# Turning the first up block of each MLP by transposing transfers that start from SBUF

## The chip, the cores and the metric

The program runs on one NeuronCore of a Trainium2 chip. The metric is device time in microseconds from the start to the end of one execution, taken as the median over runs; lower is better. Five engines work side by side, each through its own list of instructions in order: PE (TensorE, matrix products), ACT (ScalarE), DVE (VectorE), POOL (GpSimd) and SP (SyncE, which here only issues transfers). Transfers are also issued by POOL. They are carried out by 16 DMA engines.

## The reference, cut to what matters

The reference is a two-layer decoder trunk on 256 rows (tokens) of 2048 values: attention, cross attention into 256 memory rows, and an MLP per layer, each on a normalised input and added to a residual stream. The change touches the MLP alone:

```python
D_MODEL, SEQ, DEPTH, D_FF = 2048, 256, 2, 4 * 2048

def sq_relu_mlp(h, wup, wdown):
    return jnp.square(jax.nn.relu(h @ wup)) @ wdown

x = x + sq_relu_mlp(rms_norm(x, mlp_norm[i]), mlp_wup[i], mlp_wdown[i])
```

All values are 32-bit floats.

## The kernel before, in words

**Products.** Every matrix product is made of three reduced-precision products: a 32-bit operand is split into a high half (a cast, on ACT) and a low half (operand minus high half, on DVE), and PE adds high·high, high·low and low·high into PSUM. So every weight tile of 128 x 2048 words that lands in a buffer called `raw` passes through ACT (`whi`, L221) and DVE (`wlo`, L222), in two pieces of 1024, before PE can use it. There are seven raw buffers, and four buffers each for the high and the low pieces, so ACT and DVE can be at most four pieces ahead of PE.

**Weight transfers.** The raw tiles are loaded on SP's queue in program order (`load`, L189). Some tiles get a second tile added by an accumulating transfer on POOL's queue (L879). A helper, `tc.keep_in_program_order`, ties an instruction to its place in its own queue.

**The MLP.** The 8192 hidden columns are cut into eight blocks of 1024, each of two halves of 512. Of block 0 both halves are made by plain products: an "up" chunk has four items (four raw tiles, 24 matmuls of 128x512 each) and its result stands in two PSUM banks called `mm`, one per row tile t of 128 rows. Blocks 1 to 7 are made with Strassen's scheme, seven products instead of eight (`Seven`; PSUM banks called `pr`; each product p1 to p7 has two items x0 and x1 of 12 matmuls). A "down" item multiplies a finished hidden half by one raw tile of the second weight (24 matmuls).

**The order on PE.** PE's list is written out by hand and kept as it is. `mlp_line` (from L1131) makes it: items of `Seven` in a fixed order, and between them, at the places that `SPREAD` names, items of block 0's second half and down items of finished blocks. A down item may be placed only when the hidden half that it reads counts as usable. Around block 1 the list reads: p1x0, p1x1, up item 0 (second half of block 0), p5x0, p5x1, up 1, p6x0, up 2, p3x0, p6x1, up 3, p3x1, then the first down item, which reads the first half of block 0, then p2x0, and the second down item, which reads the second half. The second half counts as usable 6 places after its last up item.

**The order on the other engines.** ACT, DVE, POOL and SP get their order from a scheduler that plays the program forward with its own estimates; the program gives it tasks that say, by a number after `yield`, how long to wait before the next step is put into the program.

**From an up chunk to a down item.** The hidden values leave PSUM with rows on the partitions and must be turned so that hidden columns are on the partitions. `out` (L1450) does it for one row tile and half: Relu with the row's scale, a square (L1457, L1458, both ACT), then one of two ways. One goes through memory: ACT copies the 512 words into two planes of 16-bit halves (`half_words`, L377), POOL stores the planes to HBM (L379), SP issues a transposing transfer back into SBUF (`turned_by_dma`, L384), which puts the two 16-bit halves of a word side by side again, and ACT and DVE split the landed words into high and low halves (`split_landed`, L390, L391). The other goes through PE: four 128x128 transposes into a PSUM bank (`transpose4`, which calls `flip`, L174), then `split` (L366, L367). Before the change the first half of block 0 takes the way through memory, and the second half takes the way through PE. Each half has two row tiles, and there are two layers, so each way is used four times.

Of the kernel before, what the change touches and what calls it, by code (L numbers as in the profile page):

```python
# [10 lines left out]
F32 = mybir.dt.float32  # L11
F32R = mybir.dt.float32r
I32 = mybir.dt.int32
U16 = mybir.dt.uint16
# [4 lines left out]
P = 128  # L19
# [3 lines left out]
CH = 512  # L23
# [4 lines left out]
LAST = MLP_BLOCKS - 1  # L28
SEVEN = (1, 2, 3, 4, 5, 6, 7)
SPREAD = {("p1", 1), ("p5", 1), ("p6", 0), ("p6", 1), ("p2", 0), ("p2", 1), ("p7", 1)}  # L30
EVS = 7
# [3 lines left out]
T_EV, T_TURN, T_ROT, T_SM, T_SQ, T_ADD, T_NORM, T_SUM, T_BATCH, T_STORE, T_LAND, T_DMA, T_SHORT = 2.6, 2.6, 12.0, 6.5, 4.4, 2.2, 7.2, 3.0, 17.0, 22.0, 7.0, 8.0, 11.0  # L35

URGENT = 250
NEG = -1.0e30
LAMBDA_INIT = 0.8 - 0.6 * math.exp(-0.3 * 0)
SC_DA = 1.0 / math.sqrt(128)  # L40
# [12 lines left out]
def trunk(ctx, tc, x, xT, xT0, mem, memT, positions, gcols, gfinal, lam_vecs, consts, W, out):  # L53
    nc = tc.nc

    def pool(name, bufs, space=None):
        kw = {"space": space} if space else {}
        return ctx.enter_context(tc.tile_pool(name=name, bufs=bufs, **kw))
# [5 lines left out]
    work = pool("work", 2)  # L64
# [6 lines left out]
    def nm(s):  # L71
        serial[0] += 1
        return f"{s}_{serial[0]}"

    def unit():
        return units.tile([P, 2, 4, S], F32R, tag="unit", name=nm("unit"))
# [79 lines left out]
    def side_bank():  # L156
        while not free_banks[0]:
            yield 0.5
        free_banks[0] -= 1
        return bank()  # L160

    def give_back():
        free_banks[0] += 1
# [12 lines left out]
    def f32(ap):  # L176
        return ap.bitcast(F32)
# [6 lines left out]
    def urgent():  # L184

        return tc.high_priority(offset=URGENT)

# [174 lines left out]
    def split(dst, t, src):  # L362

        n = src.shape[1]
        hi = dst[:, 0, :n, t * P : (t + 1) * P]
        nc.scalar.copy(hi, src)  # L366
        nc.vector.tensor_tensor(dst[:, 1, :n, t * P : (t + 1) * P], src, f32(hi), ALU.subtract)  # L367
# [7 lines left out]
    def half_words(src):  # L375
        planes = work.tile([P, 2, CH], U16, tag="ev", name=nm("planes"), padded_shape=[P, 2, CH], bufs=EVS)
        nc.scalar.copy(planes, src.bitcast(U16).rearrange("p (w s) -> p s w", s=2))  # L377
        there = turned.tile([2 * P, CH], U16, tag="turned", name=nm("turned"))
        nc.gpsimd.dma_start(there.rearrange("(q s) w -> q s w", s=2), planes)  # L379
        return there  # L380

    def turned_by_dma(there):
        landed = work.tile([P, 4, 2 * P], U16, tag="ev", name=nm("landed"), bufs=EVS)
        tc.keep_in_program_order(nc.sync.dma_start_transpose(landed, there))  # L384
        return landed.bitcast(F32).rearrange("p k t -> p k t")

    def split_landed(dst, t, src):
        at = slice(t * P, (t + 1) * P)
        hi = dst[:, 0, :, at]
        tc.keep_in_program_order(nc.scalar.copy(hi, src))  # L390
        nc.vector.tensor_tensor(dst[:, 1, :, at], src, f32(hi), ALU.subtract)  # L391

    def transpose4(src, pt):

        for k in range(4):
            flip(pt[:, k * P : (k + 1) * P], src[:, k * P : (k + 1) * P])
        return pt.rearrange("p (k t) -> p k t", k=4)
# [711 lines left out]
    def mlp_line(l):  # L1109

        def up(b, h):
            return Chunk(l, "up", [(b, h)]).items()

        def both(b, *more):
            return [(b, 0), (b, 1), *more]

        groups = [both(b) for b in range(MLP_BLOCKS)]

        def down(i):
            pairs = ((0, 1), (2, 3)) if (LAST - i) % 2 == 0 else ((2, 3), (0, 1))
            chunks = [Chunk(l, "down", groups[i], c, open=i == 0) for c in pairs[0]]
            chunks += [Chunk(l, "down", groups[i], c, close=False) for c in pairs[1] if i < LAST - 2 or c == 3]
            return [i for c in chunks for i in c.items()]

        line = up(0, 0)
        rest = up(0, 1) + [i for b in range(LAST - 1) for i in down(b)]
        seven = [i for b in SEVEN for i in Seven(l, b).items()]

        usable = {(0, 0): 0}  # L1131
        now, owed = 0, 0
        for item in seven:
            line.append(item)
            now += 1
            b = item.of.b
            if item.u == ("p4", 1):
                usable.update({(b, h): now + 6 for h in range(2)})
            owed += item.u in SPREAD or (b, item.u) == (1, ("p3", 1))
            while owed and rest:  # L1140
                of, u = rest[0].of, rest[0].u
                if of.kind == "down" and usable.get(of.halves[u], math.inf) > now:
                    break
                if of.kind == "up" and u == 3:
                    usable[of.halves[0]] = now + 6
                line.append(rest.pop(0))
                now += 2
                owed -= 1
        assert not rest
        plain = [  # L1150
            i
            for c in (3, 0, 1, 2)
            for i in Chunk(l, "down", both(LAST - 2, *both(LAST - 1)) if c == 2 else both(LAST - 1), c, open=c != 3).items()
        ]
        forms = {}
        pairs = {k: Pair(f"mlp_wdown{l}", 8 * LAST, 2, c, forms) for k, c in (("A", (0, 1)), ("B", (2, 3)))}
        end = []
        at = {}
        for word in CLOSING.split():
            at[word] = len(end)  # L1160
            if word == "u":
                end.append(plain.pop(0))
            else:
                of, p = pairs[word[0]], "p" + word[1]
                end.append(Item(of, p, [of.job(p)]))
        assert not plain
        steps = {}

        def put(i, do):
            steps.setdefault(i, []).append(do)  # L1170

        pairs["B"].by_sides = l == 1
        put(0, lambda hid: pairs["A"].sums([k for c in range(2) for k in hid[LAST, c].tasks]))
        for k, of in pairs.items():
            put(max(0, at[k + "1"] - 3), lambda hid, of=of: of.fetch("t", of.home()))
            put(at[k + "1"] - 1, lambda hid, of=of: of.step("p1"))
        for p in ("p5", "p6", "p3"):
            for k, of in pairs.items():
                put(at[k + p[1]] - 3, lambda hid, of=of, p=p: of.step(p))
        for i, todo in steps.items():  # L1180
            end[i].early = lambda hid, todo=todo: [do(hid) for do in todo]
        return line, end, pairs["A"]

    mlp_lines = {l: mlp_line(l) for l in range(2)}

    forms = {}
# [252 lines left out]
    def mlp(l, norm, gnext):  # L1439
# [10 lines left out]
        def out(b, c, t, src, r, wait):  # L1450

            if (b, c) not in hid:
                hid[b, c] = Held(unit())
            dst = hid[b, c]

            def task():
                nc.scalar.activation(r, src, AF.Relu, scale=rstd[t])  # L1457
                nc.scalar.activation(r, r, AF.Square)  # L1458
                if b < LAST and (b, c) != (0, 1):
                    mine = [half_words(r), None]  # L1460
                    if b == 0:
                        yield T_STORE
                        mine[1] = turned_by_dma(mine[0])
                    elif (c, t) == (0, 1):
                        yield T_BATCH + (10.0 if b == LAST - 1 else 0.0)
                        for other in turning.pop(b):
                            other[1] = turned_by_dma(other[0])
                        yield T_STORE - T_BATCH
                        mine[1] = turned_by_dma(mine[0])
                    else:  # L1470
                        turning.setdefault(b, []).append(mine)
                        while mine[1] is None:
                            yield 0.7
                    yield T_LAND
                    split_landed(dst, t, mine[1])
                    yield T_DMA
                    return
                yield wait
                pt = yield from side_bank()
                pt = transpose4(r, pt)  # L1480
                if b < LAST or (t, c) != (1, 0):
                    split(dst, t, pt)
                if b == LAST:
                    pair.keep(t, c, pt)
                yield T_TURN
                give_back()

            dst.run(task())
# [43 lines left out]
        line, end, pair = mlp_lines[l]  # L1532
# [305 lines left out]
def _layout(i):  # L1838
# [16 lines left out]
    c[:, C_ID : C_ID + P] = np.eye(P, dtype=np.float32)  # L1855
    c[:, C_MASK : C_MASK + P] = np.where(q[None, :] <= q[:, None], 0.0, NEG)
    inv = [500000.0 ** (-(np.arange(0, r, 2)) / r) for r in (DA_ROT, MLA_ROPE)]
# [49 lines left out]
```

## Time and profile before

| | |
|---|---|
| median of 3 runs | 2170.71 us (2169.35 to 2171.35) |
| span of the profiled execution, first to last instruction | 2169.0 us (no other time of that execution is given) |
| PE busy | 2155.4 us, 99% of the span |
| DVE busy | 1740.2 us, 80% |
| ACT busy | 1465.6 us, 68% |
| POOL busy | 221.0 us, 10% |
| granted PE clock, mean | 0.999 |
| chain of waits that ended last | PE 95%, DVE 3%, DMA 1%, issue 1% |

Busy time of an engine is the time in which it has an instruction under way. PE's matmuls overlap: each lasts about 0.39 us in the profile while one starts every 0.23 us, so distances between starts are what counts. An instruction's idle time stands in brackets behind it, with the engine and instruction that ended it. A transfer's "time to landing" runs from its issue on a queue to its completion. The trace has no row for the time at which a transfer's data begin to move.

### The profile page before, as it was taken

To read this page: it belongs to the slowest core of one execution; us is meant where nothing else is said; L and a number is where in the kernel's file an instruction comes from. 1 tells how busy PE (TensorE), PEld (TensorE's weight loads), DVE (VectorE), ACT (ScalarE), POOL (GpSimd) and SP (SyncE) were. 2 spreads that over 40 slices of the span, in tenths; PEclk is the share of its full clock that TensorE was granted. 3 is DMA by queue.
4 is the path that set the end of the run, shared out by engine and by line. 5 is a ranking of instruction groups with operands and counts; after the bars stand their busy time and mean duration, and the time that the engine had idled before them with its cause. 6 is when DMAs were issued, how large, how long until landed. Compare 5 with 4: busy or idle time off the path is not lost.

```text
span 2169.0 us, 27519 instructions
## 1 busy us (share of the span) xinstructions
PE 2155.4 (99%) x10187; PEld 1805.5 (83%) x10187; DVE 1740.2 (80%) x1962; ACT 1465.6 (68%) x1938; POOL 221.0 (10%) x336
## 2 busy tenths in 40 slices
PE   9999999999999999999999999999999999999998
PEld 7888888888888888888889988888888888888887
DVE  6656878788788889788886878778888888888887
ACT  7556756666767777776665755666777778677665
POOL 1113210001000000000000420000000000000001
PEclk9999999999999999999999999999999999999999
DMA  9477896548989999998986344645998999999895
GB/s 386 151 248 234 260 293 222 194 151 267 297 280 267 308 282 256 319 274 260 306 251 218 103 170 155 221 168 182 283 299 292 258 317 280 266 285 310 254 315 149
DMA packets 151863, 543.89 MB, mean 251 GB/s; under 512 B 79536, under 2 KB 79920, under 8 KB 92848
## 3 DMA queue, kind: packets, MB, share of 16 engines
q1 hardware_dynamic: 134496, 440.14, 56.9%
q0 software_dynamic: 16800, 101.20, 22.5%
q8 instruction: 80, 1.31, 0.2%
q10 hardware_dynamic: 432, 0.79, 0.1%
q14 instruction: 55, 0.45, 0.1%
HBM read 505.38 MB, written 19.40 MB: 242 GB/s over the span
## 4 chain that ended last, share of the span: by engine, by line
PE 95%; DVE 3%; DMA 1%; issue 1%; ACT 0%; DVEq 0%; POOLq 0%; POOL 0%
PE mm L170 62%; PE pr L170 28%; PE ax L170 3%; DVE wlo L222 1%; DMA raw<-in_mlp_wup_dram 1%; PE ax L174 1%; PE mm L174 1%; DVE raw L887 0%; DVE unit L391 0%; ACT whi L221 0%; DVE x L545 0%; DMA raw<-in_da_wqkv_dram 0%; PE pr L174 0%; DVE p L680 0%; DVE ev L1722 0%
## 5 line engine op out<-in xcount | busy, mean ns | idle before, releaser
L222 DVE TENSOR_TENSOR wlo<-raw,whi 128x1024 fp32r<-128x1024 f32 (+3 forms) x946 | 1138.8, 1217 | 335.5 <-ACT whi L221 313.7
L221 ACT CAST whi<-raw 128x1024 fp32r<-128x1024 f32 (+2 forms) x945 | 985.3, 1045 | 576.8 <-PE mm L170 420.0
L170 PE MATMUL mm<-whi,unit 128*128 128x512 f32 (+2 forms) x4000 | 1271.2, 389 | 1.3 <-DVE unit L391 0.9
L170 PEld LDWEIGHTS mm<-whi,unit 128*128 128x128 f32 x4000 | 749.1, 188 | 149.6 <-DVE unit L391 1.7
L170 PE MATMUL mm<-wlo,unit 128*128 128x512 f32 (+2 forms) x2000 | 774.1, 387 | 0.2
L170 PE MATMUL pr<-whi,unit 128*128 128x512 f32 x1912 | 610.5, 389 | 0.0
L170 PEld LDWEIGHTS mm<-wlo,unit 128*128 128x128 f32 x2000 | 376.2, 188 | 72.8 <-DVE wlo L222 3.0
L170 PEld LDWEIGHTS pr<-whi,unit 128*128 128x128 f32 x1912 | 358.8, 188 | 73.4
L170 PE MATMUL pr<-wlo,unit 128*128 128x512 f32 x956 | 372.3, 389 | 1.5 <-DVE wlo L222 1.5
L170 PEld LDWEIGHTS pr<-wlo,unit 128*128 128x128 f32 x956 | 179.7, 188 | 40.0 <-DVE wlo L222 3.6
L379 POOL DMA_DIRECT2D turned<-planes x66 | 37.7, 572 | 673.5 <-ACT planes L377 661.2
L887 DVE TENSOR_TENSOR raw<-raw,raw 128x2048 f32<-128x2048 f32 x40 | 91.5, 2288 | 8.8 <-DMA raw<-in_mlp_wup_dram 8.6
L545 DVE TENSOR_TENSOR x<-x,mm 128x512 f32<-128x512 f32 x128 | 85.3, 682 | 14.1 <-PE mm L170 14.0
L879 POOL DMA_DIRECT2D raw<-in_mlp_wup_dram x48 | 43.4, 905 | 447.8 <-DVE wlo L222 445.2
L431 POOL TENSOR_TENSOR rs<-rs,mhalf 128x1 f32<-128x1 f32 (+1 forms) x26 | 24.9, 962 | 408.1 <-DVE rs L430 408.0
L222 DVE TENSOR_TENSOR wlo<-unit,whi 128x1024 fp32r<-128x1024 f32 x48 | 57.3, 1221 | 5.2 <-ACT whi L221 4.0
L221 ACT CAST whi<-unit 128x1024 fp32r<-128x1024 f32 x48 | 49.8, 1053 | 9.7 <-PE pr L170 9.7
L377 ACT COPY planes<-p 128x1024 uint16<-128x1024 uint16 x48 | 50.0, 1041 | 0.3
L170 PE MATMUL mm<-unit,whi 128*128 128x256 f32 x256 | 46.9, 285 | 0.0
L425 ACT ACTIVATE junk<-x 128x512 bf16<-128x512 f32 (+1 forms) x57 | 35.3, 620 | 10.1 <-DVE x L1092 5.0
L1457 ACT ACTIVATE p<-p,r 128x512 f32<-128x512 f32 x42 | 30.4, 724 | 16.4 <-DVE p L962 7.4
L170 PEld LDWEIGHTS mm<-unit,whi 128*128 128x128 f32 x256 | 40.2, 192 | 0.3
(199 smaller groups left out, 1280.7 us busy)
## 6 DMA issues: line engine op xcount, KB each, us to landing
raw<-in_mlp_wdown_dram SPq DMA_DIRECT2D x128, 1024.0 KB, 7.3
raw<-in_mlp_wup_dram SPq DMA_DIRECT2D x120, 1024.0 KB, 6.9
raw<-in_mlp_wup_dram POOLq DMA_DIRECT2D x48, 1024.0 KB, 9.1
raw<-in_da_wqkv_dram SPq DMA_DIRECT2D x45, 1024.0 KB, 9.8
turned<-planes POOLq DMA_DIRECT2D x66, 256.0 KB, 6.4
raw<-in_da_wo_dram SPq DMA_DIRECT2D x16, 1024.0 KB, 7.0
raw<-in_ca_wkv_dram SPq DMA_DIRECT2D x16, 1024.0 KB, 6.7
raw<-in_mlp_wdown_dram POOLq DMA_DIRECT2D x16, 1024.0 KB, 10.7
```

What stands on the lines that cost most here:

```text
L170: return nc.tensor.matmul(o, stationary, moving, start=start, stop=stop, skip_group_check=onto)
L174: nc.tensor.transpose(o, src, ident)
L221: nc.scalar.copy(hi, r)
L222: nc.vector.tensor_tensor(lo, r, f32(hi), ALU.subtract)
L377: nc.scalar.copy(planes, src.bitcast(U16).rearrange("p (w s) -> p s w", s=2))
L379: nc.gpsimd.dma_start(there.rearrange("(q s) w -> q s w", s=2), planes)
L425: return nc.scalar.activation(junk[:, : src.shape[1]], src, AF.Square, scale=scale, accum_out=acc)
L431: nc.gpsimd.tensor_tensor(r[:, :n], r[:, :n], mhalf.broadcast_to([P, n]), ALU.pow)
L545: nc.vector.tensor_tensor(xc, xc, ps, ALU.add)
L879: tc.keep_in_program_order(nc.gpsimd.dma_start(onto, src, accum_op=ALU.add))
L887: nc.vector.tensor_tensor(o, o, q, ALU.add)
L1457: nc.scalar.activation(r, src, AF.Relu, scale=rstd[t])
```

## The change

Both halves of block 0 take a third way, in both layers. After Relu and square, ACT copies the 512 words of a row tile into two planes of 16-bit halves, laid out one after the other in the row (`parted`). SP issues one transposing transfer from those planes in SBUF straight into the buffer that held the hidden values (`turned_here`): eight blocks of 128x128, four per plane. The planes land apart, so ACT copies them back into words, low and high 16 bits interleaved, over the first planes buffer (`joined`). Then `split_landed` as before. There is no store to HBM, and no PE transpose for block 0. The scheduler's task waits 6.4 of its units between the planes and the transfer and 4.6 between the transfer and the joining copy. In `mlp_line` the second half counts as usable 8 places after its last up item instead of 6. Other blocks keep their ways; the two conditions that are simplified at the end of the diff leave what they do for those blocks unchanged.

```diff
@@ -35,6 +35,7 @@
+T_PART, T_JOIN = 5.0, 4.6
@@ -383,6 +384,28 @@
+    def parted(src):
+        n = src.shape[1]
+        planes = work.tile([P, 2 * n], U16, tag="ev", name=nm("planes"), padded_shape=[P, 2 * CH], bufs=EVS)
+        nc.scalar.copy(planes.rearrange("p (s w) -> p s w", s=2), src.bitcast(U16).rearrange("p (w s) -> p s w", s=2))
+        return planes
+
+    def turned_here(planes, onto=None):
+        n = planes.shape[1]
+        if onto is None:
+            onto = work.tile([P, n], U16, tag="ev", name=nm("landed"), padded_shape=[P, 2 * CH], bufs=EVS)
+        else:
+            onto = onto.bitcast(U16)
+        landed = onto.rearrange("p (n t) -> p n t", t=P)
+        tc.keep_in_program_order(nc.sync.dma_start_transpose(landed, planes))
+        return landed
+
+    def joined(landed, planes):
+        n = landed.shape[1] // 2
+        words = planes.rearrange("p (k t s) -> p s k t", s=2, t=P)
+        nc.scalar.copy(words, landed.rearrange("p (s k) t -> p s k t", s=2))
+        return planes.bitcast(F32).rearrange("p (k t) -> p k t", t=P)
@@ -1142,7 +1165,7 @@
-                    usable[of.halves[0]] = now + 6
+                    usable[of.halves[0]] = now + 8
@@ -1456,12 +1479,17 @@
             def task():
                 nc.scalar.activation(r, src, AF.Relu, scale=rstd[t])
                 nc.scalar.activation(r, r, AF.Square)
-                if b < LAST and (b, c) != (0, 1):
+                if b == 0:
+                    planes = parted(r)
+                    yield T_SQ + 2.0
+                    landed = turned_here(planes, r)
+                    yield T_JOIN
+                    split_landed(dst, t, joined(landed, planes))
+                    yield T_TURN
+                    return
+                if b < LAST:
                     mine = [half_words(r), None]
-                    if b == 0:
-                        yield T_STORE
-                        mine[1] = turned_by_dma(mine[0])
-                    elif (c, t) == (0, 1):
+                    if (c, t) == (0, 1):
@@ -1478,10 +1506,9 @@
-                if b < LAST or (t, c) != (1, 0):
+                if (t, c) != (1, 0):
                     split(dst, t, pt)
-                if b == LAST:
-                    pair.keep(t, c, pt)
+                pair.keep(t, c, pt)
```

In the changed program the new lines stand at L391 (planes), L401 (transfer), L407 (joining copy), L413 and L414 (split); lines that the rest of this text calls L170, L221, L222, L887 are one to 23 further down there.

## The prediction

> **What bounds the kernel now.** I read the page's busy times and its chain first, then who waited for whom on PE, then the order of time around block 0 of layer 0.
>
> ```profile
> span 2169.0 us, 27519 instructions
> PE 2155.4 (99%) x10187; PEld 1805.5 (83%) x10187; DVE 1740.2 (80%) x1962; ACT 1465.6 (68%) x1938; POOL 221.0 (10%) x336
> PE mm L170 <- DVE unit L391: 0.9, 2, 0.5
> ```
>
> PE is idle for 2169.0 - 2155.4 = 13.6 us in all. Whatever takes work off PE is gained nearly whole, and a stall put on PE is lost whole, since no idle time is left to make it up. Of PE's waits (us in total, times, longest), the one shown lies in the stretch that changes, once per layer: the first down item waits for the split of block 0's first half. In layer 0, PE's list and the chain read:
>
> ```profile
> 547.61 0.39 PE L170 MATMUL mm<-whi,unit 128*128 128x512 f32 x1
> 547.83 0.39 PE L170 MATMUL mm<-wlo,unit 128*128 128x512 f32 x1
> 548.67 0.74 PE L170 MATMUL mm<-whi,unit 128*128 128x512 f32 x2 [0.45 <-DVE unit L391]
> ...
> 551.27 0.44 PE ax L174 x4
> ...
> 555.83 0.44 PE ax L174 x4
> ```
>
> Starts 547.83 and 548.67 lie 0.84 us apart; one start per 0.23 us is the rule (547.83 against 547.61 for the matmul ahead), so 0.61 us is lost. Four PE transposes take 0.44 us of the path.
>
> **What it removes.** Per layer two groups of four transposes, 2 x 0.44 = 0.88 us, and, if the first half is split long before its down item, the 0.61 us. Together 1.5 us per layer, **-3.0 us** for both: the most that PE's rows offer here. POOL loses four stores off the path, and the bank copies of L366 and L367 become L413 and L414 of the same kind.
>
> **What it adds.** ACT's list, before and then changed, from the first planes copy of the first half (`planes_4679`, row tile 0; `planes_4684` is row tile 1; `unit_4676` is the turned half):
>
> ```order
> L377 COPY planes_4686<-ev_4683 128x1024
> L954 COPY p_968_4738<-pr_4690 128x512
> L221 CAST whi_4691<-raw_4508 128x1024
> L221 CAST whi_4695<-raw_4508 128x1024
> L221 CAST whi_4715<-raw_4713 128x1024
> L221 CAST whi_4719<-raw_4713 128x1024
> ```
>
> ```order
> L407 COPY planes_4679<-ev_4675 128x2x512
> L222 CAST whi_4641<-unit_4432 128x1024
> L391 COPY planes_4684<-ev_4681 128x1024
> L977 COPY p_966_4734<-pr_4686 128x512
> L413 CAST unit_4676<-planes_4679 128x4x128
> L222 CAST whi_4687<-raw_4508 128x1024
> L222 CAST whi_4691<-raw_4508 128x1024
> L407 COPY planes_4684<-ev_4681 128x2x512
> L222 CAST whi_4711<-raw_4709 128x1024
> L413 CAST unit_4676<-planes_4684 128x4x128
> ```
>
> The joining copies (L407) now stand in ACT's list ahead of casts of weights: when a transfer has not landed, ACT stands still, and every cast behind it, DVE's low halves and PE wait too. SP's list at the same place, before and changed (`raw_4713` and `raw_4709` are the same tile, that of up item 1):
>
> ```order
> L189 DMA raw_4713<-in_mlp_wup_dram 128x2048
> L189 DMA raw_4779<-in_mlp_wup_dram 128x2048
> L189 DMA raw_4804<-in_mlp_wup_dram 128x2048
> L189 DMA raw_4862<-in_mlp_wup_dram 128x2048
> L384 DMA_TRANSPOSE landed_4878<-turned_4681 128x4x256
> ```
>
> ```order
> L190 DMA raw_4709<-in_mlp_wup_dram 128x2048
> L401 DMA_TRANSPOSE ev_4675<-planes_4679 128x8x128
> L401 DMA_TRANSPOSE ev_4681<-planes_4684 128x8x128
> L190 DMA raw_4777<-in_mlp_wup_dram 128x2048
> L190 DMA raw_4808<-in_mlp_wup_dram 128x2048
> ```
>
> The first two transfers move ahead of three loads, but stay behind the load of up item 1.
>
> **When the first transfer lands.** Issues on SP, with the answers on time to landing for the stretches that begin at 501, 507, 513 and 521 us:
>
> ```profile
> 501.82 0.33 SPq L189 DMA_DIRECT2D raw<-in_mlp_wup_dram  x1
> raw<-in_mlp_wup_dram SPq DMA_DIRECT2D x1, 1024.0 KB, 10.9
> ...
> 507.03 0.33 SPq L189 DMA_DIRECT2D raw<-in_mlp_wup_dram  x1
> raw<-in_mlp_wup_dram SPq DMA_DIRECT2D x1, 1024.0 KB, 14.2
> ...
> 513.81 2.23 SPq L384 DMA_TRANSPOSE landed<-turned  x1
> landed<-turned SPq DMA_TRANSPOSE x1, 8.1
> ...
> 521.03 1.23 SPq L384 DMA_TRANSPOSE landed<-turned  x1
> landed<-turned SPq DMA_TRANSPOSE x1, 3.1
> ```
>
> The load issued at 507.03 landed at 521.2, the transfer issued at 513.81 at 521.9, 0.7 us behind it; the one at 521.03, with SP's queue empty, took 3.1. So SP's queue hands its data over in order. Load 501.82 lands at 512.7, and that part does not change. The planes for the first transfer are done at 506.7, but it lands only behind that load: 512.7 + 0.7 = 513.4, or 0.7 earlier, as a store that shared the engines is gone. I take **513.0**. A transfer from SBUF has no row: below, it can be no faster than behind its queue (512.7); above, it takes longer than one from HBM by an unknown amount, a case of its own below.
>
> **What that does to PE.** ACT and DVE before, and the start of p5x0 on PE:
>
> ```profile
> 505.65 1.04 ACT L377 COPY planes<-ev 128x1024 uint16<-128x1024 uint16 x1
> ...
> 509.59 1.99 ACT L221 CAST whi<-unit 128x1024 fp32r<-128x1024 f32 x2
> 511.49 1.04 ACT L377 COPY planes<-ev 128x1024 uint16<-128x1024 uint16 x1
> 512.43 0.58 ACT L954 COPY p<-pr 128x512 f32<-128x512 f32 x1
> 512.91 1.05 ACT L221 CAST whi<-raw 128x1024 fp32r<-128x1024 f32 x1
> ```
>
> ```profile
> 510.67 2.36 DVE L222 TENSOR_TENSOR wlo<-unit,whi 128x1024 fp32r<-128x1024 f32 x2
> 513.06 2.29 DVE L887 TENSOR_TENSOR unit<-unit,raw 128x2048 f32<-128x2048 f32 x1
> 515.27 3.57 DVE L222 TENSOR_TENSOR wlo<-raw,whi 128x1024 fp32r<-128x1024 f32 x3
> 514.97 0.39 PE L170 MATMUL pr<-whi,unit 128*128 128x512 f32 x1
> ```
>
> p5x0 starts at 514.97, 12 matmuls later (2.72 us) p5x1, whose second matmul needs its low piece: 517.92. Before, that piece was ready at about 516.5. Now let J be the start of the first joining copy. Its price has no row; it handles 1024 two-byte values as the planes copy does, so between 0.6 (a cast of 512 words, L390 below) and twice 1.04, and I take 1.0. ACT then goes on, 1.0 each: cast of p5x0's second piece to J + 2.0, planes of row tile 1 to 3.0, L954 to 3.5, L413 to 4.1, cast of p5x1's first piece to 5.1. DVE is in order too: low piece of p5x0 from J + 2.05 to 3.3, the 2.29 us addition (L887) to 5.6, L414 to 6.2, and only then the low piece of p5x1, ready at J + 7.4. With J = 513.0 that is 520.4 against 517.92: PE stands for **2.5 us**. It begins to cost from J = 510.5. The second joining copy costs nothing more: its transfer is issued at J + 3.1 on an empty queue, lands 3.1 later, and ACT gets to it at J + 6.1. The loads issued between 501.82 and 507.03 now leave SP at about 518 (J + 3.1, and the 1.2 to 2.2 us that issuing a transfer takes), some 12 us late; the first is up item 2's, wanted on PE at 528.6 (514.97 plus 60 starts), and on an empty queue 1 MB has had time to land by then.
>
> **The second half.** ACT's changed list from the planes of row tile 0 (`planes_5006`); `raw_4707` is p7x0, `raw_4968` p2x1, `raw_5044` the second down item:
>
> ```order
> L222 CAST whi_4950<-raw_4921 128x1024
> L1481 ACTIVATE ev_5008<-ev_5008 128x512
> L1480 ACTIVATE p_1008_4966<-p_1008_4966,r_926_4502 128x512
> L407 COPY planes_5006<-ev_5002 128x2x512
> L391 COPY planes_5011<-ev_5008 128x1024
> L222 CAST whi_4970<-raw_4707 128x1024
> L1481 ACTIVATE p_1008_4966<-p_1008_4966 128x512
> L413 CAST unit_5003<-planes_5006 128x4x128
> L222 CAST whi_4974<-raw_4707 128x1024
> L378 COPY planes_5038<-p_1008_4966 128x1024
> L222 CAST whi_5014<-raw_4968 128x1024
> L407 COPY planes_5011<-ev_5008 128x2x512
> ```
>
> Here too casts have moved behind a wait, and PE, with the second down item two places later, takes p2x0, p7x0 and p2x1 in a row: six pieces 1.36 us apart, from 553.1 on (547.6, the first down item's start, plus 24 starts). The stretch before:
>
> ```profile
> 545.09 1.06 ACT L221 CAST whi<-raw 128x1024 fp32r<-128x1024 f32 x1
> 546.04 1.13 ACT L390 CAST unit<-landed 128x512 fp32r<-128x512 f32 x2
> ...
> 547.66 1.99 ACT L221 CAST whi<-raw 128x1024 fp32r<-128x1024 f32 x2
> 549.55 0.63 ACT L1458 ACTIVATE ev<-ev 128x512 f32<-128x512 f32 x1
> 550.08 0.71 ACT L1457 ACTIVATE p<-p,r 128x512 f32<-128x512 f32 x1
> 542.37 0.91 POOL L879 DMA_DIRECT2D raw<-in_mlp_wup_dram  x1 [8.20 <-DVE wlo L222]
> raw<-in_mlp_wup_dram POOLq DMA_DIRECT2D x1, 1024.0 KB, 8.3
> ```
>
> The planes copy takes the place of the two L390 casts, so the transfer is issued at 547.1, beside POOL's load that lands at 550.7, and lands 3.1 to 4.5 later (the upper end is an estimate: 3.1 doubled for the part that shares). The joining copy starts at K = 550.8 to 551.6. In ACT's order, 0.6 to 1.0 each, p2x1's second piece is cast at K + 9.2 and its low half ready at K + 10.4; PE wants it at 553.1 + 5 x 1.36 + 0.23 = 560.1. That is 1.1 to 1.9 us late, and the casts of p7x0 on the way already eat most of it; the split of row tile 1 may add 0.6. I take **1.7 us**, with 0 and 3.9 (K = 553) as ends.
>
> **Sum.** Per layer +2.5 + 1.7 - 1.5 = +2.7; two layers alike, **+5.4 us**. The profiled span 2169.0 becomes 2174.4; the median lies 1.7 above that span, so **2176**.
>
> **The rivals.**
>
> *All hidden.* The joins find their data landed, and only the 3.0 us come off: 2167.7. It needs J below 510.5, with the load ahead landing at 512.7; for it speaks that ACT is 68% busy and that pieces could be ready earlier than my steps of 1.0. It would hold from a slack of 2.5 us more than I count. Part of that leaves the time within a few us of before.
>
> *The transfer from SBUF is slow in itself.* If it takes 6 us alone, J = 515.9 (5.4 us at p5x1), the second join waits until J + 9.1 and the casts behind it bring the stall to 7.7 at up item 1; the second half costs some 4.4. Per layer 12.1 - 1.5, so 2192. Against it: it has as many bytes as one from HBM, which took 0.7 us behind a load. On this case the Trainium skill, "VectorE: DVE Perf Modes", section "Rules for kernel authors", advises TensorE for a 128x128 transpose if PSUM will do, and the transfer otherwise; its table gives 1309 ns by transfer. Eight such blocks in a row would be 10.5 us, an estimate from that page, and the sum would pass 2192; the 3.1 us of the trace for as many blocks speaks against that size, though not against the advice.
>
> *The change does not do what it says*, in that a load or a semaphore moved with it costs or spares PE a wait somewhere else: within 2 us of 2170.7.
>
> **How the numbers follow.** About 0.2%, 4.3 us, is what a measurement can tell from no change. Forecast 0.55 (of it 0.42 above 4.3 us, 0.13 below, as J and K vary); all hidden 0.25 (0.22 within, 0.03 faster by finding more than my 3.0); slow transfer 0.13, all slower; other 0.07 (0.05 within, 0.02 faster). So faster 0.05, within 0.40, slower 0.55. The ends: 2167.7, all hidden; J = 514.5 and K = 552.5 give 4.0 + 2.8 - 1.5 = 5.3 per layer, 2181.3, and some of the slow transfer's weight takes it to 2183. Range 2167.5 to 2183.
>
> **What would show it.** Right: L174 in 16 fewer matmuls; L407 on ACT idle until a transfer lands near 513 in layer 0; PE waiting for L223 (the low pieces) by some 2.5 us near 518 and 1 to 2 us near 558 in each layer; no wait for L414 at the first down item. Wrong: transfers from SBUF landing in over 5 us on an empty queue, landing ahead of the load issued before them, or PE without new waits while the joins are late, which would mean that ACT had more pieces in hand than I count.

## The result and the profile after

The changed kernel takes 2183.72 us, the median of four runs (2182.79 to 2184.69), against 2171.03 us of the kernel before beside it (2169.35 to 2172.36). The ratio is 1.0059, with a 95% interval of 1.0047 to 1.0071: slower by 12.7 us. The prediction said 2176, and at most 2183.

The page of the changed kernel, its first line and its busy times:

```profile
span 2181.0 us, 27488 instructions
PE 2160.9 (99%) x10171; PEld 1803.7 (83%) x10171; DVE 1739.8 (80%) x1962; ACT 1477.0 (68%) x1950; POOL 218.6 (10%) x332
```

PE has 16 instructions fewer, as announced, and yet 5.5 us more busy time (2160.9 against 2155.4), beside 6.5 us more idle time. Idle time was foreseen; a PE that is longer busy with less to do was not. What PE waited for (us in total, times, longest), of which the kernel before had 1.5 us for the low pieces and none for ACT's casts:

```profile
PE pr L171 <- DVE wlo L223: 7.9, 12, 1.9
PE pr L171 <- ACT whi L222: 1.2, 4, 0.4
```

No wait for L414 is left: the first down item finds its half split. In layer 0, the first half, in order of time (start, duration, engine, line, and in brackets the idle time before and what ended it), first ACT, then DVE, then PE:

```profile
513.07 1.35 ACT L407 COPY planes<-ev 128x1024 uint16<-128x1024 uint16 x1 [2.36 <-DMA ev<-planes]
...
516.62 2.29 DVE L910 TENSOR_TENSOR unit<-unit,raw 128x2048 f32<-128x2048 f32 x1
518.83 0.68 DVE L414 TENSOR_TENSOR unit<-planes,unit 128x512 fp32r<-128x512 f32 x1
519.43 3.49 DVE L223 TENSOR_TENSOR wlo<-raw,whi 128x1024 fp32r<-128x1024 f32 x3
...
518.28 0.50 PE L171 MATMUL pr<-whi,unit 128*128 128x512 f32 x1 [0.22 <-ACT whi L222]
520.70 0.64 PE L171 MATMUL pr<-wlo,unit 128*128 128x512 f32 x1 [1.92 <-DVE wlo L223]
521.14 1.05 PE L171 MATMUL pr<-whi,unit 128*128 128x512 f32 x2
521.99 0.63 PE L171 MATMUL pr<-wlo,unit 128*128 128x512 f32 x1
```

The joining copy waits for its transfer until 513.07, DVE comes to p5x1's low piece after its addition and L414, and PE stands until 520.70. But then three matmuls take 1.29 us (521.99 less 520.70), where 0.69 is the rule. Stretches of 3.41 us from the same trace, of layer 0 and then of layer 1, show why. The columns are the stretch, its length, then busy time and count of PE, PEld, DVE, ACT and POOL, the granted PE clock, the share of the DMA engines and GB/s:

```profile
514.09:517.50 3.41, 3.41 (x16) 2.61 (x16) 2.11 (x2) 3.41 (x6) 0.00 (x0) 1.00 0.00 0
517.50:520.91 3.41, 1.27 (x5) 0.52 (x4) 3.41 (x4) 3.16 (x4) 0.00 (x0) 1.00 0.93 216
520.91:524.32 3.41, 3.41 (x9) 2.64 (x9) 3.41 (x4) 3.22 (x4) 0.00 (x0) 0.50 1.02 430
524.32:527.73 3.41, 3.41 (x17) 2.79 (x16) 3.00 (x4) 1.53 (x2) 0.00 (x0) 1.00 1.02 430
...
1541.50:1544.91 3.41, 1.72 (x6) 0.83 (x5) 3.41 (x3) 3.16 (x4) 0.00 (x0) 1.00 0.81 187
1544.91:1548.32 3.41, 2.97 (x7) 2.40 (x8) 3.41 (x5) 3.31 (x5) 0.00 (x0) 0.50 1.00 413
```

Behind the stall the clock is at half for exactly one stretch of 3.41 us, in both layers. In layer 0 that is 1.7 us of work lost, more than half of the stall again; in layer 1, where PE still stands at the start of that stretch, it is 1.5.

The second half, ACT and PE:

```profile
557.61 1.35 ACT L407 COPY planes<-ev 128x1024 uint16<-128x1024 uint16 x1 [2.36 <-DMA ev<-planes]
...
560.86 0.51 PE L171 MATMUL pr<-whi,unit 128*128 128x512 f32 x1 [0.40 <-ACT whi L222]
562.12 0.51 PE L171 MATMUL pr<-wlo,unit 128*128 128x512 f32 x1 [0.76 <-DVE wlo L223]
564.11 0.50 PE L171 MATMUL pr<-wlo,unit 128*128 128x512 f32 x1 [0.32 <-DVE wlo L223]
```

How late PE is at each place can be read from an instruction that both traces have. The first matmul of up item 1 starts at 520.41 before and at 524.92 after. The first addition of block 0's result to the residual stream in layer 0, on DVE, stands in the two traces (before, then after):

```profile
648.84 0.69 DVE L545 TENSOR_TENSOR x<-x,mm 128x512 f32<-128x512 f32 x1 [1.40 <-PE mm L170]
```

```profile
655.36 0.69 DVE L568 TENSOR_TENSOR x<-x,mm 128x512 f32<-128x512 f32 x1 [1.40 <-PE mm L171]
```

So 6.5 us are lost by then. How they divide shows when one adds up, between 515 and 570, how much later than 0.23 us after the one ahead each start on PE comes, leaving out delays under 0.05: 2.7 at the first stall, 1.7 by half clock, 3.6 in the second half, together 8.0, less the 1.5 saved. Layer 1 loses another 6.2. The rest of the program gives 0.7 back (a wait of 1.25 us near 1014 in the profile before is not in the one after, and small ones are added); such waits come and go between profiles of one and the same order.

### The profile page after: what moved, and what is told of

It reads as the page before. It is cut to its first block, busy times and chain, and to the rows that moved or that the text cites. A ratio compares the mean times of both kernels' runs of the same rounds, so it can differ in the third digit from the quotient of the medians.

```text
span 2181.0 us, 27488 instructions
## 1 busy us (share of the span) xinstructions
PE 2160.9 (99%) x10171; PEld 1803.7 (83%) x10171; DVE 1739.8 (80%) x1962; ACT 1477.0 (68%) x1950; POOL 218.6 (10%) x332
## 3 DMA queue, kind: packets, MB, share of 16 engines
q8 instruction: 79, 1.29, 0.2%
## 4 chain that ended last, share of the span: by engine, by line
PE 93%; DVE 2%; DMA 1%; issue 1%; ACT 1%; DVEq 0%; POOLq 0%; POOL 0%; ACTq 0%
PE mm L171 61%; PE pr L171 27%; PE ax L171 3%; DVE wlo L223 1%; DMA ev<-planes 1%; PE ax L175 1%; PE mm L175 1%; ACT whi L222 1%; DVE unit L414 0%; DVE x L568 0%; DMA raw<-in_mlp_wup_dram 0%; ACT planes L391 0%; PE ax L1267 0%; DVE raw L910 0%; ACT planes L407 0%
## 5 line engine op out<-in xcount | busy, mean ns | idle before, releaser
L222 ACT CAST whi<-raw 128x1024 fp32r<-128x1024 f32 (+2 forms) x945 | 983.8, 1044 | 570.4 <-PE mm L171 410.4
L222 ACT CAST whi<-unit 128x1024 fp32r<-128x1024 f32 x48 | 49.9, 1052 | 10.2 <-PE pr L171 10.1
```

Source lines behind the costliest of these rows:

```text
L222: nc.scalar.copy(hi, r)
```

## The experiments

Each was timed beside the kernel before; "price" is PE's time lost per layer in the profile against the kernel before. Where a kernel inserts lines, line numbers move by a few.

### The halves apart

```diff
-                if b == 0:
+                if (b, c) == (0, 0):      # first half alone; second as before, usable 6 places later
...
+                if (b, c) == (0, 1):      # second half alone; first as before, usable 8 places later
```

First half alone:

> The first half alone goes by transposing transfers out of SBUF; the second half is turned on TensorE as in the kernel before and is used 6 places later, as before. Theory (the copies of ScalarE that wait for a transfer hold up the pieces of the next up item; and the idle time of some 2.2 us on TensorE that follows is itself followed by 3.4 us at half the granted clock): the first half keeps its whole price, 4.45 us per layer in the changed kernel's trace, and there is no gain but the wait of 0.61 us of the first down item at most, so +3.8 to +4.45 per layer: 2178.7 to 2180. The clock reads 0.50 for three 1-us windows near 521 and near 1545. Rival (the second half is the dear one, the first only shifts its start): below 2175.

Second half alone:

> The second half alone goes by transposing transfers out of SBUF and is used 8 places later; the first half goes through HBM as in the kernel before. Theory: no wait near 518 to 521 and a clock of 1.00 throughout; the waits of 0.1 to 1.0 us between 555 and 563 stay, 2 to 3 us per layer, less the eight transposes of TensorE (0.88 per layer) : 2173 to 2175.5. Rival (the second half's waits come only from the lateness that the first half leaves on SP's queue and on ScalarE): no waits there, 2169 to 2170.

**Measured.** The first half alone takes 2178.44 us, ratio 1.0032 (1.0021 to 1.0044), 0.3 us under the expected range. The second alone takes 2184.01, ratio 1.0053 (1.0040 to 1.0067), as much as both together, and both expectations for it fall: to the waits for low pieces comes one of 2.07 us in layer 0 and 1.64 in layer 1 for the half's own split, at the down item that reads it, and half clock behind it in layer 0. More on this below. The other surprise: the first half alone has the same stall in both layers, and the clock falls in only one of them.

```profile
516.53:519.94 3.41, 1.95 (x7) 1.05 (x6) 3.41 (x3) 3.15 (x5) 0.00 (x0) 1.00 0.69 123
519.94:523.35 3.41, 2.73 (x12) 2.28 (x13) 3.41 (x4) 3.41 (x5) 0.00 (x0) 1.00 1.00 413
...
1540.53:1543.94 3.41, 1.28 (x5) 0.53 (x4) 3.41 (x4) 3.15 (x4) 0.00 (x0) 1.00 0.97 216
1543.94:1547.35 3.41, 3.41 (x9) 2.67 (x10) 3.41 (x4) 3.27 (x4) 0.00 (x0) 0.50 1.03 432
```

These stretches are not chosen freely. In each trace the times at which the clock changes lie on a grid of 3.413 us (in the changed kernel 520.91 and 1544.91 lie 300 times 3.4133 us apart), and the grid lies differently in every execution. In layer 0 of this run a grid line at 519.94 cuts the stall in two, PE is busy 1.95 us in the one part, and the clock stays. In layer 1 one stretch holds the whole stall, PE is busy 1.28 us in it, and the next runs at half clock. The six runs fall apart: four at 2177.5 to 2178.5 with a mean clock of 0.998, two at 2181.4 and 2182.7 with 0.997. A second stretch at half clock fits the clock of those two, but no trace of them was kept, and its 1.7 us would not fill the gap of 2.9; the kernel before, timed beside them, spreads from 2169.87 to 2175.05 without any such stall.

### Work in the stall

```diff
                     mmul(o, form[:, 0, kk], wh, kk == 0 and on == p, False, on != p)
+                    if (self.b, p, kk) == (1, "p5", 4):
+                        spare = bank("ax")
+                        for _ in range(9):
+                            nc.tensor.matmul(spare, identr, form[:, 0, 0:4], start=True, stop=True)
```

On the changed kernel:

> The changed kernel, with nine extra matmuls (128x512) into a bank that nothing reads, put in each layer behind the first matmul of the piece of the first up item that waits; the output does not change. They fill about 2 us of the 2.2 us in which TensorE waits there and cost nothing else if they fit in. Theory (the idle time brings the half clock): the granted clock stays 1.00 from 521 to 525, the matmuls start 0.23 us apart, and 1.5 to 2.1 us per layer come back: 2179.5 to 2181. Rival (the half pace comes from the four weight loads that run at 400 to 430 GB/s at the same time, or from power, not from idle time): the clock still reads 0.50 there, and the time stays at 2183 to 2185.

On the first half alone:

> The first half alone from SBUF with its joins where the change has them, with the nine extra matmuls per layer in the stall; the output does not change. Theory (a window of 3.41 us in which TensorE stands idle for some 2 us is followed by one at half clock; whether one window holds the whole stall changes from run to run): the clock stays at 1.00, all runs lie close together, and at 2.2 to 2.5 us per layer over the kernel before: 2175.5 to 2177, where the runs without the extra matmuls lay at 2177.5 to 2178.5 with one such window and at 2181.4 to 2182.7 with more. Rival (the half clock comes from the loads that follow, or by chance): windows at half clock as before, 2177.5 to 2183.

**Measured.** In both kernels the clock stays at 1.00 through the stall of both layers, with the loads behind it as dense as ever. Here is layer 0 of the changed kernel with the nine matmuls:

```profile
517.94:521.35 3.41, 3.21 (x14) 2.10 (x13) 3.41 (x4) 3.17 (x4) 0.00 (x0) 1.00 1.00 260
521.35:524.76 3.41, 3.41 (x16) 2.81 (x15) 3.41 (x4) 3.41 (x5) 0.00 (x0) 1.00 1.00 411
```

So it is PE's own idleness, and not the loads, that halves the clock. First half alone: 2177.06 (2175.31 to 2179.52), ratio 1.0025 (1.0016 to 1.0034), where it was 1.0032 without the extra matmuls; just above the expected range. All eleven runs have a mean clock of 0.999, where those without have 0.997 or 0.998; but they do not lie close together, as was expected, and spread by 4.2 us. The changed kernel comes to 2183.19, ratio 1.0050 (1.0038 to 1.0063). Against 1.0059 that is 2 us less, with intervals that overlap: the theory's clock, but not its 1.5 to 2.1 us per layer. In its trace PE loses 0.9 us less in each of the two layers: the half clock's 1.7 and 1.5 are back, and a part goes into new short gaps of 0.1 to 0.3 us around the stall and behind it. Even so the span of this profile is 2181.5 us, against 2181.0, since other waits between and behind the two MLPs are longer in it; what of these is chance was not tested.

### The first half's copies later

```diff
-        nc.scalar.copy(words, landed.rearrange("p (s k) t -> p s k t", s=2))
+        copy = nc.scalar.copy(words, landed.rearrange("p (s k) t -> p s k t", s=2))
+        if pin:                              # pin: c == 0
+            tc.keep_in_program_order(copy)
...
-                    yield T_JOIN
+                    yield 10.0 if c == 0 else T_JOIN
```

On the changed kernel:

> The changed kernel with the first half's two joining copies put some ten to fifteen instructions later on ScalarE (behind the casts of the next pieces), and the subtractions of VectorE that read them with them; all else as in the change. Theory (the first half's price is the place of its joining copies on ScalarE): no wait near 518 to 521, clock 1.00, 4.45 us per layer come back: 2174 to 2176. Rival (the transfers themselves, or their place on SP's queue ahead of the weight loads, are what costs): not below 2181.

On the first half alone:

> The first half alone from SBUF, with its joining copies put later on ScalarE; the second half turned on TensorE as before. It differs from the run with the first half alone only in the places of two copies and of what follows them on each layer. Theory (the price of the first half is the place of these copies and nothing else): all of the 2.2 to 4.0 us per layer goes, no window at half clock, and the time is that of the kernel before, 2170 to 2172. Rival (part of the price is the place of the transfers on SP's queue, or the strided write of the copies itself): 2174 or more.

**Measured.** The joining copies now run near 535 and 538 and wait for nothing. First half alone: **2169.46 us (2167.72 to 2172.61), ratio 0.9991 (0.9982 to 1.0000)**. The whole price is gone, so the first half's cost was the place of two copies in ACT's list, with the splits that follow them, and nothing else. PE's waits in it, of all lines the three longest:

```profile
PE ax L1269 <- DVE coef L1357: 1.2, 1, 1.2
PE ax L175 <- DVE ev L1752: 0.7, 2, 0.5
PE pr L171 <- DVE wlo L223: 0.4, 2, 0.2
```

The changed kernel comes to 2177.99, ratio 1.0028 (1.0017 to 1.0039): some 7 us less than without, of the 9 that the theory said, because the second half took some of it back. Its copy waits longer (3.25 us for 2.36), the transfer being bound to something other than PE, and in layer 0 the half clock has moved there:

```profile
554.42 1.35 ACT L407 COPY planes<-ev 128x1024 uint16<-128x1024 uint16 x1 [3.25 <-DMA ev<-planes]
```

```profile
555.69:559.10 3.41, 1.38 (x6) 0.60 (x5) 1.45 (x2) 3.41 (x6) 0.00 (x0) 1.00 0.39 74
559.10:562.51 3.41, 3.41 (x9) 2.65 (x10) 2.58 (x3) 3.41 (x4) 0.58 (x1) 0.50 0.95 311
```

### What the second half's transfer waits for

The kernel leaves out, once per layer, the accumulating load on POOL's queue that runs beside the second half's first transfer, and with it one addition to a weight tile.

```diff
-                    self.fetch(0, 1, x, o)
+                    if (self.b, x) != (1, 1):
+                        self.fetch(0, 1, x, o)
```

On the kernel with the first half's copies later:

> The kernel with the first half's joins later, less one transfer: the accumulating load of POOL (1 MB into the raw tile of the piece p3x1 of the first up item) is left out in each layer, so that its output differs; the order of the instructions on TensorE, VectorE and ScalarE is the same. Theory (the second half's first transfer lands 5.9 to 6.9 us after it is issued, since its packets stand behind that load's on the DMA engines; 3.0 us on empty ones): it lands in 3.0 to 4 us, the joining copy of the second half no longer waits 3.25 us, and the second half's price falls by 2.5 to 3.5 us per layer (and the half clock with it): 2170 to 2173. Rival (the transfer is slow by its own 1024 small packets or by the engines that read SBUF): it still lands after 6 us and the time stays at 2177 to 2179.

**Measured.** 2172.07, ratio 1.0005 (0.9996 to 1.0014): with this one load gone, all of the change's cost is gone. Time from issue to landing of all transfers out of SBUF (min, median, max), with POOL's load and without:

```profile
DMA to landing us min/median/max: 3.0/4.7/6.8
```

```profile
DMA to landing us min/median/max: 3.0/3.1/6.4
```

The second half's first transfer, which took 6.8 us, takes 3.0 (the 6.4 is the first half's, behind SP's load). Its joining copy starts at 551.17 without a wait, and PE loses 1.2 us in the second half. In the kernel with it POOL's load was issued at 544.99 (8.4 us to landing) and the transfer on SP's queue at 547.57, when SP's own load ahead had landed (issued at 541.71, 4.9 us to landing). That is two queues, and still the transfer lands at 554.4, some 1 us behind POOL's load. No row gives a single transfer's start, but the packets that each queue moved can be counted by stretch (packets, MB, share of 16 engines; q0 is POOL's queue, q1 SP's), from 547.5 to 551 and from 552 to 553:

```profile
q0 software_dynamic: 79, 0.65, 92.7%
...
q1 hardware_dynamic: 478, 0.12, 80.6%
q0 software_dynamic: 18, 0.02, 12.8%
```

In the first stretch SP's queue moves no packet, though the transfer was issued in it: it stands until POOL's load is nearly through. A load less could spare time of its own; the run further down, in which the same load is left out beside the second half alone and the ratio goes from 1.0053 to 1.0048 only, speaks against that as the reason.

### Both halves later

The joining copies of both halves go further back on ACT, and the second half is used 12 or 14 places after its last up item.

```diff
-                    usable[of.halves[0]] = now + 8
+                    usable[of.halves[0]] = now + 12          # 14 in the third
...
-                    yield T_JOIN
+                    yield 14.0 if c == 0 else T_JOIN         # 9.0 for c == 1 in the second and third
...
+                    split_landed(dst, t, joined(landed, planes, True))
```

> The changed kernel with the joining copies of both halves put later on ScalarE (the first half's behind the casts of the pieces of the next up item, the second half's some ten instructions later), and with the second half used 12 places later instead of 8. Theory (what costs is that the copies stand on ScalarE ahead of casts that TensorE needs, before their transfers have landed): both stalls gone and no window at half clock, so 3.0 us below the kernel before (1.5 per layer): a ratio of 0.9986, about 2168 to 2170. Rival (transfers out of SBUF cost by their place on SP's queue, ahead of the weight loads of the next items, wherever the copies stand): a wait for a load takes the stalls' place, 2174 or more.

> As the run with both joins later and the second half used 12 places later, with the second half's joining copies another five instructions later on ScalarE. Theory: the same time as that run if its second half no longer waits; up to 2 us per layer less if its copies are still ahead of their transfers (which land 6 to 7 us after they are issued). Rival (place on SP's queue): the same time, 2174 or more.

> As the run before (second half's joining copies latest), with the second half used 14 places later. Theory: the same as with 12 places if the copies land in time for the first down item; if that item waits for ScalarE's unit (as it did, 2.07 and 1.64 us, where the second half alone went from SBUF), 1.6 to 2.7 us per layer less than with 12. Rival: slower, because the down items that are put off collide with the next block's: over 2172.

**Measured.** 2185.42, ratio 1.0075 (1.0054 to 1.0096); 2189.38, 1.0088 (1.0075 to 1.0101); 2204.07, 1.0156 (1.0143 to 1.0169). The later, the worse, and the theory fails on time, though no joining copy waits for its transfer any more. New waits took their place. The longest of PE's in the first (us in total, times, longest):

```profile
PE mm L171 <- DVE wlo L223: 5.8, 6, 2.6
PE pr L171 <- DVE p L987: 3.8, 2, 1.9
```

in the second:

```profile
PE mm L171 <- ACT unit L415: 8.9, 2, 4.4
PE pr L171 <- ACT p L1483: 3.8, 2, 1.9
```

and in the third:

```profile
PE pr L171 <- ACT whi L222: 20.4, 2, 10.4
```

When down items go later, products of the scheme come sooner: PE waits 1.9 us per layer for a `pr` bank that DVE is still reading (L987; in the second and third the profile puts the same wait down to ACT's L1483, which does not read that bank), and in the second for a half that is split too late (L415). The longest waits of the first and the third stand behind loads, as the rival has it. DVE in the first, and ACT in the third:

```profile
610.90 2.29 DVE L912 TENSOR_TENSOR raw<-raw,raw 128x2048 f32<-128x2048 f32 x1 [2.65 <-DMA raw<-in_mlp_wup_dram]
```

```profile
587.83 1.99 ACT L222 CAST whi<-unit 128x1024 fp32r<-128x1024 f32 x2 [6.47 <-DMA unit<-in_mlp_wup_dram]
```

Why these loads come late, by the transfers' place or by the later down items, was not separated. The second and the third differ in nothing but the place of the half's use, and two places later cost 15 us more.

### The second half in other orders

The second half alone, without POOL's load (as above), and then also with its second transfer sooner:

```diff
-                    yield T_SQ + 2.0
+                    yield T_SQ + 2.0 if t == 0 else T_SQ
```

> The second half alone from SBUF, less the one accumulating load of POOL per layer (the piece p3x1 of the first up item), so that its output differs; the order on TensorE, VectorE and ScalarE is that of the run with the second half alone. Theory (the second half's price, 4.7 us per layer and 1.7 more with a window at half clock, is its first transfer waiting behind that load): the price goes down to the ScalarE's own extra work, 2170 to 2173. Rival (the first down item waits for the second half's second transfer in any case, 2.07 and 1.64 us): 2176 or more.

> The second half alone from SBUF, less POOL's accumulating load (so that the output differs), as in the run before it of that kind, with its second transfer put into the program two units sooner: the second planes copy stands ahead of the first joining copy on ScalarE, and SP's queue is no longer held for 10 us behind it. New theory (what was left of that kernel's price is the second transfer at the head of SP's queue, waiting for its planes copy, with the down items' loads behind it): no wait of ScalarE for a down item's load near 564, no wait of TensorE for ScalarE's unit near 566, no half clock, 2170 to 2174. Rival (the second half is used too early with 8 places, wherever its transfers are issued): 2179 to 2183.

The same edit, for the second half only, on the kernel with the first half's copies later, with nothing left out:

> The kernel with the first half's joins later, and with the second half's second transfer put into the program two units of the scheduler's time sooner, so that both planes copies of the second half stand on ScalarE ahead of both joining copies, and its two transfers are issued one behind the other near 552 us, when POOL's accumulating load has landed. Nothing is left out. Theory (the second half's price is a joining copy that waits, on ScalarE, for a transfer that stands behind POOL's load, with all that is queued behind the copy): no window at half clock, the waits for VectorE's low pieces near 558 to 565 fall from 4.2 to 1 to 2.5 us per layer, 2170 to 2174. Rival (the second half has its price wherever its copies stand, as the run with both joins later suggests): 2177 or more.

**Measured.** The second half alone without POOL's load: 2182.57, ratio 1.0048 (1.0035 to 1.0062). Both its transfers land in 3.1 us at most, and it is hardly faster, so here the load is not the cause. ACT and PE in it:

```profile
564.54 1.04 ACT L222 CAST whi<-raw 128x1024 fp32r<-128x1024 f32 x1 [1.42 <-DMA raw<-in_mlp_wdown_dram]
...
566.16 0.50 PE L171 MATMUL mm<-whi,unit 128*128 128x512 f32 x1 [1.65 <-ACT unit L413]
```

SP's queue stood from 548.3 to 558.4 on the two transfers, because the planes copy for the second one ran only at 556.08; the down items' loads came behind it, and the cast that waits for one stands in ACT's list ahead of the split that PE waits for. With the second transfer sooner the load's wait is gone, and the time is 2178.45, ratio 1.0030 (1.0018 to 1.0042): between the two expectations. PE still waits 2.4 us for the split, since in that order the joining copy of row tile 0, which PE needs first, comes last. The complete kernel with that edit takes 2175.93, ratio 1.0026 (1.0017 to 1.0035), which cannot be told from the 1.0028 without it, and lies between the two expectations. Its second half's transfers land in 3.2 us, as the theory wanted, and PE still waits, now for what is queued on ACT:

```profile
PE pr L171 <- DVE wlo L223: 2.7, 5, 0.8
PE pr L171 <- ACT whi L222: 1.7, 2, 0.8
PE mm L171 <- DVE unit L416: 1.0, 1, 1.0
```

In every complete kernel tried here the second half costs PE more than the 0.9 us per layer that its transposes took. That there is no order in which it would cost less is not shown, and what each copy on ACT costs there is left open.

## Why the prediction was wrong, step by step

| per layer, us | predicted | measured in layer 0 |
|---|---|---|
| transposes and first down item's wait saved | -1.5 | -1.5 |
| first stall | +2.5 | +2.7 |
| half clock behind it | 0 | +1.7 |
| second half | +1.7 (0 to 3.9) | +3.6 |
| sum | +2.7 | +6.5 |

**Right: the gains, and the first stall with its chain.** J was taken as 513.0 and is 513.07, and the low piece, predicted for 520.4, lets PE go on at 520.70. That J came so near is in part luck: the load ahead landed at 512.0 instead of 512.7, and the transfer 1.05 us behind it instead of at most 0.7. The run with the first half's copies later shows the mechanism: with the transfers at their places in SP's list and only the copies moved, nothing is lost. The copy's price of 1.0, between 0.6 and 2.08, is 1.35.

**Failed: "a stall put on PE is lost whole".** In layer 0 it is lost 1.6 times over. The prediction priced a stall at its length and let PE go on at 0.23 us per matmul; the granted clock was read as one mean for the whole program (0.999) and never asked what it does behind a stall. No stall of this size stood in the profile before, where PE waits 1.2 us at most at one time; but the end of that profile, where PE's work runs out within a stretch, has the same drop:

```profile
2159.49:2162.90 3.41, 0.88 (x8) 0.67 (x6) 2.29 (x6) 2.14 (x7) 0.55 (x1) 1.00 0.71 261
2162.90:2166.31 3.41, 0.00 (x0) 0.00 (x0) 1.00 (x2) 0.92 (x2) 0.00 (x0) 0.50 0.82 294
```

The nine matmuls in the stall show that idleness is the cause.

**Mis-sized: the second half, through K.** The prediction took K = 550.8 to 551.6 for the start of the second half's first joining copy and 553 for the end of its range. Measured it is 557.61, less the 3.9 us by which PE was late there: 553.7. The failing part is "3.1 doubled for the part that shares". The transfer did not share with POOL's load; it landed behind it, 5.9 us after its issue. So the second half cost 3.6 us instead of 1.7. With that load taken away the copy starts at 551.17, and the second half costs 1.2 us, inside the 1.1 to 1.9 that the working gave for that K. The steps from K to PE were right, and the duration put into them was not.

**The rivals.** *All hidden* did not happen with the change as it stands, but it is what the first half does once its copies stand later: 2169.46 against the 2167.7 worked out for both halves. *The transfer from SBUF is slow in itself* is refuted: on an empty queue it lands after 3.0 us, like the one from HBM (3.1), and the Trainium skill's 1309 ns per 128x128 block, from "VectorE: DVE Perf Modes", "The three transpose paths", would have made 10.5 for eight in a row, an estimate from that page. The advice of that page's "Rules for kernel authors", TensorE for a 128x128 transpose if PSUM will do, holds for the second half in every complete kernel tried here, though not for the reason of the transfer's own duration. *The change does not do what it says* did not happen either: the waits stand where the change put them.

**The range.** Its upper end, 2183, was built from later J and K (2181.3) and some weight of the slow transfer, with nothing for the clock, and lies 0.7 us below the result. Half clock in both layers, 3.2 us, would have held it.

## What to carry to other kernels

A copy that waits for a transfer belongs in its engine's list where the transfer has surely landed, with something behind it that can wait; here moving two copies per layer by 16 and 12 places was worth all of the first half's 7 us, while putting the use of the data from 12 to 14 places only cost more. When PE has no slack, price a stall of about 2 us with up to another 1.7 for the clock, and reckon that a transfer issued just behind a 1 MB load may land behind it even from another queue, as it did here. And part of a stall that is removed may be paid again at the next wait whose end does not depend on PE.

## What the runs showed of the hardware

**The clock goes by a grid of 3.41 us and does not need an idle stretch.** In all the traces, the last 25 us of each left out, half clock followed every stretch at full clock in which PE was busy 1.53 us or less, eleven in number, and none with 1.88 or more. In between it goes both ways: it followed 1.69, 1.72, 1.77, 1.80 and 1.83 us and did not follow 1.60, 1.70, 1.72, 1.77 and 1.82. Matmul ends in these rows are modelled, so the bound, somewhere near half of the stretch, is known no better. The Trainium skill, "TensorE: Matmul & The Clock Gate", "Part 1: The HAM clock gate", describes a free-running window of 3413 ns, which agrees with the 3.41 us of these traces, and half rate after an idle window; its section "HAM oscillation — how this bites in real kernels" puts the rule as no idle gaps over about 3.4 us. Here a single wait of some 2 us was enough where it fell within one window, so for these traces that rule is too loose. As the grid lies differently in each execution, whether such a stall is followed by half clock can differ from one execution to the next; how much of the spread of the times comes from that was not separated.

**A transfer can land behind a load of another queue.** The transposing transfer on SP's queue, issued 2.6 us after POOL's load of 1 MB, landed behind it (6.8 us, against 3.0 without the load), though SP's queue was empty, and its packets moved only when that load was nearly through. Order of issue is no rule between queues: in the changed kernel a store that POOL issued at 564.11 landed after 7.0 us, ahead of a load that SP had issued at 562.27, behind other loads of its own, and that took 10.3.

**The joining copy is dearer than the copy that makes the planes.** It writes every second 16-bit value and takes 1.35 us; the planes copy reads every second one and takes 1.04.
